# Score matmuls of a dilated attention layer: the low parts of the keys in 128-row tiles padded with zero rows

## The chip, the core and the metric

The kernel is one program on one core of a Trainium2 chip. The metric is the device time of one execution in microseconds (us); each number below is either such a time or was read from one execution that the hardware profiler recorded. Engine names: PE is the tensor engine (PEld its weight loads), DVE the vector engine, ACT the scalar engine, POOL GpSimd, SP the queue that issues the DMAs.

## The reference, cut to what matters

A trunk of four layers on 256 tokens of width 1024. Layer i has a mixer (retention, dilated attention, gMLP, retention), a SwiGLU channel mixer and a gated embedding. Only layer 1, the dilated attention, is touched. It has 16 heads of width 64 and three groups of window and dilation; each group has queries, keys and values of its own.

```python
qkv = (h @ w_in).reshape(B, S, 3, 3, 16, 64)
for gi, (window, dil) in enumerate(((128, 1), (512, 4), (2048, 16))):
    logits = einsum('qhd,khd->hqk', q, k) * 64 ** -0.5 + bias   # masked outside the window
    e = exp(logits - max); o = e @ v / sum(e); lse = max + log(sum(e))
w = softmax(lse over the three groups)
o = sum(w * o over the three groups);  return o @ w_out
```

The three groups together are one softmax over the logits of all three groups, and the kernel computes it so.

## The kernel before, in words

**Split operands.** Every float32 operand of a product is split into a high part (rounded by ACT to the format that PE multiplies in one pass, fp32r) and a low part (the rest, by DVE). A product is then three matmuls, high x high, high x low and low x high (`mm3`, L203 to L205). The weights stream in as chunks in a fixed order: SP loads them into `raw` (L146), ACT writes `wh` (L173), DVE writes `wl` (L174). The order of instructions on each engine is the order of the program text; which chunks are split where is set by a table of small numbers (`P`), and up to eight chunks are held split.

**The attention layer.** The loop runs over eight pairs of heads. For pair i PE does four chunks of the value projection (`token_major`, 12 matmuls of 384 columns for each chunk), and for each of the three groups a projection of queries and keys (`project`, 48 matmuls of 256 columns). Between these stand the steps of the pair before: `scores` of its even head after the third value chunk, `scores` of its odd head after the fourth, then, each after one of the three projections, the transposes of the probabilities (`turn_p`, L624) and the products with the values (`values`, L636 to L646). After the loop the last pair gets the same steps between the rows of the output projection.

**One call of `scores`.** There are 16 calls, one for each head. A call makes 12 matmuls in 6 couples: three of 256 columns (the later 128 queries against all keys, one for each group) and three of 128 columns (the earlier 128 queries). A couple adds into the same accumulator:

- L585 uses 128 rows. The stationary operand is `both[hh]`, in which the head's 64 rows hold the high part of the query and the other 64 rows hold its low part; the moving operand is `high[hh]`, which holds the high part of the key twice. One matmul gives high x high and low x high.
- L586 uses 64 rows, the head's own: the high part of the query against the low part of the key.

```python
both, high, low = p["qk"][g]
pe.matmul(dst, lhsT=both[hh][:, q], rhs=high[hh][:, k], start=True, stop=False)
pe.matmul(dst, lhsT=both[hh][part, q], rhs=low[part, k], start=False, stop=True)
```

`low` is one tile for each group, in which both heads of a pair have 64 rows each; DVE writes it in `project` (L677). DVE then adds the bias and finds the extreme of each row in three steps (L595, L598, L600), ACT takes the exponentials (L605, L607), DVE normalises (L613 to L616), PE transposes.

**Bias.** `load_bias` (L576) loads [128, 3, 256] for one head at the end of the loop body, two heads a pair, into a tag `bias` with two buffers. The tile `emb` ([128, 2, 1024]) lives through all layers: it holds the embedding of a layer from `Emb.unit` (written by ACT in the mixer, L381) to the evacuation of the gate (read by DVE, L1021). During the loop over the pairs it is not in use.

Of the kernel before, what the change touches and what calls it, by code (L numbers as in the profile page):

```python
# [9 lines left out]
F32 = mybir.dt.float32  # L10
F32R = mybir.dt.float32r
# [12 lines left out]
LEAD = 6  # L24
RAWS = 4
BIG = 1.0e30
# how many chunks of the weights are split at the named places, and (mt, ft) before how many of the last rows
# of a branch its first half of the tokens is transposed
P = dict(
    mt=1, mr0=0, mr1=1, mr2=0, mr3=2, mr4=0, mr5=1, m1=0, m2=1, m3=0, m4=0, m5=1, ft=2, fr0=1, fr1=1, fr2=0,  # L30
    fr3=1, fr4=0, fr5=1, f1=0, f2=1, f3=0, f4=0, f5=1, gq0=1, gq1=1, gq2=2, g1=2, g2=1, g3=0, g4=0, g5=0,
# [1 line left out]
)  # L33


# ---- the weights in the order in which they are used, a chunk per entry:
# (name, index, first row block, row blocks, columns); a chunk lies as [128 rows][row block][column]
def _cols(name, j, c0, n, nk, blocks=8):
    return [(name, j, k, nk, ((c0, n),)) for k in range(0, blocks, nk)]

# [67 lines left out]
def trunk(ctx: ExitStack, tc: tile.TileContext, x, p_t, norm_g, gcols, wts, rel_bias, gm_ln, gm_ws, gm_bs,  # L108
          c_ident, c_flip, c_rope, c_decay, c_onehot, c_mask, c_tril, out):
    nc = tc.nc  # L110
    act, dve, pe, dma = nc.scalar, nc.vector, nc.tensor, nc.sync
# [10 lines left out]
    def ps_tile(tag="ps"):  # L122
        return (psum if tag == "ps" else accp).tile([128, 512], F32, tag=tag, name=tag)

# [1 line left out]
    chunks, groups = [], []  # L126
    for l in range(DEPTH):
        off = 0
# [69 lines left out]
        def release(self):  # L198
            released.add(self.c)

# [1 line left out]
    def mm3(ps, lh, ll, rh, rl, start, stop):  # L202
        pe.matmul(ps, lhsT=lh, rhs=rh, start=start, stop=False)  # L203
        pe.matmul(ps, lhsT=lh, rhs=rl, start=False, stop=False)  # L204
        pe.matmul(ps, lhsT=ll, rhs=rh, start=False, stop=stop)  # L205

# [1 line left out]
    ident = const.tile([128, 128], F32, name="ident")  # L208
    ones = const.tile([128, 1], F32, name="ones")
    eps = const.tile([128, 1], F32, name="eps")  # L210
# [4 lines left out]
    emb = const.tile([128, 2, D], F32, name="emb")  # L215
# [28 lines left out]
    def cut(i, n=512):  # L244
        return slice(i * n, (i + 1) * n)

# [1 line left out]
    def turn(src, dst_hi, dst_lo, k0, tt, gain=None, tag="ps", wide=False):  # L248
        if gain is None:
            ps = ps_tile(tag)  # L250
# [46 lines left out]
            pe.matmul(ps[:, tok(tt)], lhsT=ones.to_broadcast([128, 128]), rhs=r[2][tt], start=True, stop=True)  # L297
        act.activation(out=r_b[:, 0, :], in_=ps[:, 0:256], func=AF.Copy)

# [1 line left out]
    def feature_major(name):  # L301
        ps = ps_tile()
        for b in range(2):
# [10 lines left out]
            mm3(ps, a_hi[:, kk, tok(tt)], a_lo[:, kk, tok(tt)], w.hi[:, k, :], w.lo[:, k, :], kk == 0, kk == 7)  # L314

    def token_whole(ps, ws, tt, then=None):
        """all chunks of a product, the parts of the activations that come last used last."""
        nk = 8 // len(ws)
        for kk in range(8):
            a, w, k = a_hi[:, kk, tok(tt)], ws[kk // nk], kk % nk  # L320
            pe.matmul(ps, lhsT=a, rhs=w.hi[:, k, :], start=kk == 0, stop=False)  # L321
            pe.matmul(ps, lhsT=a, rhs=w.lo[:, k, :], start=False, stop=False)  # L322
        for kk in range(8):
            w, k = ws[kk // nk], kk % nk
            pe.matmul(ps, lhsT=a_lo[:, kk, tok(tt)], rhs=w.hi[:, k, :], start=False, stop=kk == 7)  # L325
            if k == nk - 1:
                w.release()
                if then is not None:
                    then()
# [31 lines left out]
    def new_acc():  # L361
        return [[ps_tile("acc") for _ in range(2)] for _ in range(2)]

# [1 line left out]
    def split_p(t):  # L365
        act.activation(out=p_hi, in_=t, func=AF.Copy)
        dve.tensor_tensor(out=p_lo, in0=t, in1=p_hi.bitcast(F32), op=ALU.subtract)
# [16 lines left out]
                for w in self.w:  # L384
                    w.release()

# [1 line left out]
    def post_norm(tt, acc, gain, r):  # L388
        s = [sm(), sm()]
        for half in range(2):  # L390
# [12 lines left out]
            dve.tensor_tensor(out=h[:, tt, cut(half)], in0=h[:, tt, cut(half)], in1=t, op=ALU.add)  # L403

    def close_branch(late, acc, gain, r, l, n):
        """late: the row chunks whose second half of the tokens is still to come."""
        new = [None, None]
        act.preload_act_table(AF.Sqrt)
        K = "m" if n == 2 else "f"
        st["rate"] = 1  # L410
        post_norm(0, acc, gain, r)
        for i, (w, z, k) in enumerate(late):
            if i == len(late) - P[K + "t"]:
                turn_h(0, l, n)
            row(w, z, k, acc, False, i == len(late) - 1, (1,))
            w.release()
            pump(P[K + "r%d" % i])
        if P[K + "t"] == 0:
            turn_h(0, l, n)
        post_norm(1, acc, gain, r)  # L420
        pump(P[K + "1"])
        st["rate"] = P[K + "2"]

        def between():
            turn_h(1, l, n, True)
            pump(P[K + "3"])
            rms_of_h((0, 1), new)
            act.preload_act_table(AF.Silu if n == 2 else AF.Sigmoid)
            pump(P[K + "4"])
            st["rate"] = P[K + "5"]  # L430

        return new, between

# [1 line left out]
    def open_mixer(l, env, t):  # L435
        st["rate"] = P["rate"]
        dma.dma_start(out=t, in_=p_t[l].rearrange("(k p) t -> p k t", p=128))
# [128 lines left out]
    def attention(l, r, between, env):  # L566
        mp = env["pool"]
        name, wout = "attn_w_in", "attn_w_out"
        zf = mp.tile([128, 8, 256], F32, name="zf")
        flip = mp.tile([128, 128], F32, name="flip")  # L570
        dma.dma_start(out=flip, in_=c_flip)

        def load_bias(hd):
            t = mp.tile([128, 3, 256], F32, tag="bias", name="bias", bufs=2)
            v = vec[0, hd, :]
            dma.dma_start(out=t, in_=bass.AP(tensor=v.tensor, offset=v.offset, ap=[[1, 128], [16 * 384, 3], [1, 256]]))  # L576
            return t

        def scores(p, hh, tag="acc"):
            part = slice(64 * hh, 64 * hh + 64)  # L580
            s1, s2, s3 = ps_tile(tag), ps_tile(tag), ps_tile(tag)

            def logits(dst, g, q, k):
                both, high, low = p["qk"][g]
                pe.matmul(dst, lhsT=both[hh][:, q], rhs=high[hh][:, k], start=True, stop=False)  # L585
                pe.matmul(dst, lhsT=both[hh][part, q], rhs=low[part, k], start=False, stop=True)  # L586

            for g in range(3):
                logits((s1[:, 0:256], s1[:, 256:512], s2[:, 0:256])[g], g, tok(1), slice(0, 256))
            for g in range(3):  # L590
                logits(s3[:, cut(g, 128)], g, tok(0), tok(0))
            pr = mp.tile([128, 3, 384], F32, tag="pr", name="pr", bufs=2)
            bias = p["bias"][hh]
            m = [sm(), sm(), sm()]
            dve.tensor_tensor_reduce(out=pr[:, 0:2, 128:384], in0=s1.rearrange("p (g k) -> p g k", g=2),  # L595
                                     in1=bias[:, 0:2, :], scale=1.0, scalar=3.0e38, op0=ALU.add, op1=ALU.min,
                                     accum_out=m[0])
            dve.tensor_tensor_reduce(out=pr[:, 2, 128:384], in0=s2[:, 0:256], in1=bias[:, 2, :], scale=1.0,  # L598
                                     scalar=m[0], op0=ALU.add, op1=ALU.min, accum_out=m[1])
            dve.tensor_tensor_reduce(out=pr[:, :, 0:128], in0=s3[:, 0:384].rearrange("p (g k) -> p g k", g=3),  # L600
                                     in1=bias[:, :, 128:256], scale=1.0, scalar=3.0e38, op0=ALU.add, op1=ALU.min,
                                     accum_out=m[2])
            pump(P[("s%d" if p["p"] else "i%d") % hh] if p["p"] < 7 else 0)
            den = sm(2)
            act.activation(out=pr[:, :, 128:384], in_=pr[:, :, 128:384], func=AF.Exp, scale=-1.0, bias=m[1],  # L605
                           accum_out=den[:, 1:2])
            act.activation(out=pr[:, :, 0:128], in_=pr[:, :, 0:128], func=AF.Exp, scale=-1.0, bias=m[2],  # L607
                           accum_out=den[:, 0:1])
            return pr, den
# [42 lines left out]
        def project(p, g):  # L652
            ps = feature_major(name)
            if p["p"] == 0 and g == 0:
                spread(r)
            qk = mp.tile([128, 512], F32, tag="qk", name="qk")
            q = qk[:, 0:256].rearrange("p (a b) -> p a b", a=2)
# [3 lines left out]
                                     in0=ps[:, 0, :].rearrange("p (a b) -> p a b", a=2), scalar=-0.125,  # L661
                                     in1=r_b[:, 0, :].rearrange("p (a b) -> p a b", a=2), op0=ALU.mult, op1=ALU.mult)
            dve.tensor_tensor(out=qk[:, 256:512], in0=ps[:, 1, :], in1=r_b[:, 0, :], op=ALU.mult)
            both = [mp.tile([128, 256], F32R, tag=f"both{g}{hh}", name="both") for hh in range(2)]
            high = [mp.tile([128, 256], F32R, tag=f"high{g}{hh}", name="high") for hh in range(2)]
            low = mp.tile([128, 256], F32R, tag=f"low{g}", name="low")
            parts = (slice(0, 64), slice(64, 128))
            for hh in range(2):
                own, other = parts[hh], parts[1 - hh]
                act.activation(out=both[hh][own, :], in_=qk[own, 0:256], func=AF.Copy)  # L670
                act.activation(out=high[hh][own, :], in_=qk[own, 256:512], func=AF.Copy)
            for hh in range(2):
                own, other = parts[hh], parts[1 - hh]
                act.activation(out=high[hh][other, :], in_=qk[own, 256:512], func=AF.Copy)
                dve.tensor_tensor(out=both[hh][other, :], in0=qk[own, 0:256], in1=both[hh][own, :].bitcast(F32),
                                  op=ALU.subtract)
                dve.tensor_tensor(out=low[own, :], in0=qk[own, 256:512], in1=high[hh][own, :].bitcast(F32),  # L677
                                  op=ALU.subtract)
            p["qk"].append((both, high, low))

# [1 line left out]
        for i in range(8):  # L682
# [14 lines left out]
            p = {"p": i, "v": v, "qk": []}  # L697
# [198 lines left out]

        return compute

# [1 line left out]
    def ffn(l, r, between, env):  # L900
        fp = env["pool"]
        name, wout = "ffn_w_in", "ffn_w_out"
# [199 lines left out]
            r, between = embed_gate(l, r, between)  # L1102


# [1 line left out]
def _consts():  # L1106
    f = np.float32
    inv = (f(10000.0) ** (-np.arange(0, 256, 2, dtype=f) / f(256))).astype(f)
# [64 lines left out]
```

## Time and profile before

| what | us |
|---|---|
| median of three runs | 1769.78 (1768.28 to 1772.07) |
| span of the profiled execution, first to last instruction | 1768.2 |
| PE busy in it | 1759.0 (99%) |
| PEld busy | 1607.0 (91%) |
| DVE busy | 1141.7 (65%) |
| ACT busy | 985.1 (56%) |

The profiled execution's own time is its span, 1768.2 us, which lies 1.6 us under the median of the runs. Busy time of PE counts modelled ends of pipelined matmuls, which overlap, so a share of 99% says that PE hardly ever waits and not that each matmul goes as fast as it could. The distance from one matmul's start to the next one's, the pitch, tells more. PEclk in a view by stretches is the clock that was granted to the tensor engine, as a share of full speed (1.00 is 2.4 GHz, 0.50 is 1.2 GHz).

### The profile page before, as it was taken

The numbers are of one execution on the slowest core, as the hardware profiler recorded it, in microseconds if no ns is written. First come the engines' busy times: TensorE is split into PE (matmuls) and PEld (weight loads), VectorE is DVE, ScalarE is ACT, GpSimd is POOL, SyncE is SP. The second block draws the span as 40 slices with busy tenths as digits, with TensorE's granted clock in tenths as the row PEclk, the third lists the DMA queues.
The fourth block names the chain that finished last, engine by engine and source line by source line (L and its number), as shares of the span: only waits on it lengthen the run. The fifth ranks groups of instructions, "written<-read, shape, count | busy, mean of one in ns | idle before, by whom it ended". The sixth has DMA issues, their size and how long they took to land.

```text
span 1768.2 us, 27679 instructions
## 1 busy us (share of the span) xinstructions
PE 1759.0 (99%) x11411; PEld 1607.0 (91%) x11411; DVE 1141.7 (65%) x1670; ACT 985.1 (56%) x1515; POOL 0.2 (0%) x4
## 2 busy tenths in 40 slices
PE   9999999999999999999999999999999999999999
PEld 7888898999999999899999888899999888899998
DVE  7666665558777777775556775665557756675546
ACT  5645754348665656574445754654457555664435
POOL 0000000000000000000000000000000000000000
PEclk9999999999999999999999999999999999999999
DMA  7554564544545445356554654455545455455550
GB/s 288 210 190 155 180 218 166 206 162 169 173 148 138 144 149 162 92 192 212 182 188 167 224 195 184 167 205 200 183 164 182 175 186 183 174 203 192 179 202 24
DMA packets 53598, 314.32 MB, mean 178 GB/s; under 512 B 5632, under 2 KB 13616, under 8 KB 19168
## 3 DMA queue, kind: packets, MB, share of 16 engines
q1 hardware_dynamic: 53472, 312.56, 51.6%
q8 instruction: 89, 1.46, 0.3%
q14 instruction: 37, 0.30, 0.1%
HBM read 311.41 MB, written 1.12 MB: 177 GB/s over the span
## 4 chain that ended last, share of the span: by engine, by line
PE 96%; ACT 1%; DVE 1%; DMA 1%; issue 1%; SPq 0%; ACTq 0%; DVEq 0%
PE ps L203 21%; PE ps L204 20%; PE ps L205 20%; PE acc L203 8%; PE acc L205 8%; PE acc L204 8%; PE acc L586 1%; PE acc L585 1%; PE acc L261 1%; PE acc L624 1%; PE ps L252 1%; DMA raw<-in_w_dram 1%; PE acc L325 1%; PE acc L322 1%; PE acc L321 1%; ACT wh L173 1%
## 5 line engine op out<-in xcount | busy, mean ns | idle before, releaser
L174 DVE TENSOR_TENSOR wl<-raw,wh 128x1024 fp32r<-128x1024 f32 (+1 forms) x567 | 661.8, 1205 | 192.3 <-ACT wh L173 191.0
L173 ACT ACTIVATE wh<-raw 128x1024 fp32r<-128x1024 f32 (+1 forms) x567 | 565.3, 1040 | 178.1 <-PE ps L204 112.4
L203 PE MATMUL ps<-a_hi,wh 128*128 128x256 f32 x1792 | 514.2, 287 | 0.0
L204 PE MATMUL ps<-a_lo,wh 128*128 128x256 f32 x1792 | 510.9, 285 | 0.0
L205 PE MATMUL ps<-a_hi,wl 128*128 128x256 f32 x1792 | 510.8, 285 | 0.0
L203 PEld LDWEIGHTS ps<-a_hi,wh 128*128 128x128 f32 x1792 | 347.5, 194 | 2.6 <-issue 0.6
L204 PEld LDWEIGHTS ps<-a_lo,wh 128*128 128x128 f32 x1792 | 347.7, 194 | 1.4
L205 PEld LDWEIGHTS ps<-a_hi,wl 128*128 128x128 f32 x1792 | 347.3, 194 | 0.0
L203 PE MATMUL ps<-wh,a_hi 128*128 128x512 f32 (+2 forms) x776 | 268.6, 346 | 0.9 <-ACT wh L162 0.9
L204 PE MATMUL ps<-wl,a_hi 128*128 128x512 f32 (+2 forms) x776 | 266.7, 344 | 0.3 <-DVE wl L163 0.2
L205 PE MATMUL ps<-wh,a_lo 128*128 128x512 f32 (+2 forms) x776 | 266.6, 344 | 0.0
L203 PEld LDWEIGHTS ps<-wh,a_hi 128*128 128x128 f32 x776 | 147.5, 190 | 16.5 <-ACT wh L162 1.4
L204 PEld LDWEIGHTS ps<-wl,a_hi 128*128 128x128 f32 x776 | 147.7, 190 | 15.0 <-DVE wl L163 0.5
L205 PEld LDWEIGHTS ps<-wh,a_lo 128*128 128x128 f32 x776 | 147.8, 190 | 14.7
L203 PE MATMUL acc<-wh,hh 128*128 128x512 f32 x288 | 112.8, 392 | 0.0
L204 PE MATMUL acc<-wl,hh 128*128 128x512 f32 x288 | 112.4, 390 | 0.0
L205 PE MATMUL acc<-wh,hl 128*128 128x512 f32 x288 | 112.3, 390 | 0.0
L910 DVE TENSOR_TENSOR hid<-ps,gr 128x512 f32<-128x512 f32 x36 | 24.9, 691 | 99.6 <-PE ps L205 99.6
L913 ACT ACTIVATE hh<-hid 128x512 fp32r<-128x512 f32 x36 | 22.8, 632 | 101.7 <-DVE hid L910 101.7
L263 ACT ACTIVATE a_hi<-acc,gc 128x128 fp32r<-128x128 f32 x192 | 52.3, 382 | 39.8 <-PE acc L261 39.8
L205 PEld LDWEIGHTS acc<-wh,hl 128*128 128x128 f32 x288 | 54.1, 188 | 11.5
L203 PEld LDWEIGHTS acc<-wh,hh 128*128 128x128 f32 x288 | 54.2, 188 | 10.3
(205 smaller groups left out, 2203.4 us busy)
## 6 DMA issues: line engine op xcount, KB each, us to landing
raw<-in_w_dram SPq DMA_DIRECT2D x266, 1024.0 KB, 4.9
raw<-in_w_dram SPq DMA_DIRECT2D x16, 768.0 KB, 4.3
bias<-vec SPq DMA_DIRECT2D x16, 384.0 KB, 8.1
gain<-in_norm_g_dram SPq DMA_DIRECT2D x8, 512.0 KB, 6.7
ln<-in_gm_ln_dram SPq DMA_DIRECT2D x2, 1024.0 KB, 6.9
raw<-in_w_dram SPq DMA_DIRECT2D x3, 512.0 KB, 8.1
dec<-in_c_decay_dram SPq DMA_DIRECT2D x4, 384.0 KB, 5.6
h<-in_x_dram SPq DMA_DIRECT2D x4, 256.0 KB, 5.5
```

Source lines behind the costliest of these rows:

```text
L173: act.activation(out=hi[:, 0:n], in_=raw, func=AF.Copy)
L174: dve.tensor_tensor(out=lo[:, 0:n], in0=raw, in1=hi[:, 0:n].bitcast(F32), op=ALU.subtract)
L203: pe.matmul(ps, lhsT=lh, rhs=rh, start=start, stop=False)
L204: pe.matmul(ps, lhsT=lh, rhs=rl, start=False, stop=False)
L205: pe.matmul(ps, lhsT=ll, rhs=rh, start=False, stop=stop)
L252: pe.transpose(ps[:, cut(i, 128)], src[:, cut(i, 128)], ident)
L261: pe.transpose(ps[:, cut(i, 128)], src[:, cut(i, 128)], ident)
L263: act.activation(out=dst_hi[:, k0 + i, tok(tt)], in_=ps[:, cut(i, 128)], func=AF.Copy, scale=gain(k0 + i))
L321: pe.matmul(ps, lhsT=a, rhs=w.hi[:, k, :], start=kk == 0, stop=False)
L322: pe.matmul(ps, lhsT=a, rhs=w.lo[:, k, :], start=False, stop=False)
L910: dve.tensor_tensor(out=hd, in0=up, in1=gr, op=ALU.mult)
L913: act.activation(out=hh, in_=hd, func=AF.Copy)
```

## The change

`low` becomes `lows`: for each group and each head of a pair a tile of 128 rows, allocated once before the loop. The 64 rows that do not belong to the head are set to zero once, by six DVE memsets of 64 x 256 at the start of the layer. The second matmul of a couple then takes all 128 rows of `both[hh]`; the query's low part meets zeros. `project` writes the head's own 64 rows as before. The bias of an odd head is loaded into a part of `emb` that is not in use during the loop, and the tag `bias` has one buffer.

```diff
+        lows = [[mp.tile([128, 256], F32R, name=f"low{g}{hh}") for hh in range(2)] for g in range(3)]
+        for pair in lows:
+            for hh in range(2):
+                dve.memset(pair[hh][64 - 64 * hh:128 - 64 * hh, :].bitcast(F32), 0.0)
+
         def load_bias(hd):
-            t = mp.tile([128, 3, 256], F32, tag="bias", name="bias", bufs=2)
+            if hd % 2:
+                t = emb[:, 1, 0:768].rearrange("p (g k) -> p g k", g=3)
+            else:
+                t = mp.tile([128, 3, 256], F32, tag="bias", name="bias")
...
         def scores(p, hh, tag="acc"):
-            part = slice(64 * hh, 64 * hh + 64)
...
-                pe.matmul(dst, lhsT=both[hh][part, q], rhs=low[part, k], start=False, stop=True)
+                pe.matmul(dst, lhsT=both[hh][:, q], rhs=low[hh][:, k], start=False, stop=True)
...
-            low = mp.tile([128, 256], F32R, tag=f"low{g}", name="low")
+            low = lows[g]
...
-                dve.tensor_tensor(out=low[own, :], in0=qk[own, 256:512], in1=high[hh][own, :].bitcast(F32),
+                dve.tensor_tensor(out=low[hh][own, :], in0=qk[own, 256:512], in1=high[hh][own, :].bitcast(F32),
                                   op=ALU.subtract)
```

The rest of the diff takes comment lines out.

## Rows read from the trace of the kernel before

**Rows 1.** The profile's page: busy time of each engine; the chain that ended last.

```profile
PE 1759.0 (99%) x11411; PEld 1607.0 (91%) x11411; DVE 1141.7 (65%) x1670; ACT 985.1 (56%) x1515; POOL 0.2 (0%) x4
...
PE 96%; ACT 1%; DVE 1%; DMA 1%; issue 1%; SPq 0%; ACTq 0%; DVEq 0%
```

**Rows 2.** Waits of PE, whole span: us in total, times, longest.

```profile
PE ps L1078 <- DVE warm L1073: 1.5, 1, 1.5
```

**Rows 3.** Timeline of PE, one call of `scores`: start us, us, instruction.

```profile
697.42 0.33 PE L205 MATMUL ps<-wh,a_lo 128*128 128x384 f32 x1
697.59 0.28 PE L585 MATMUL acc<-high,both 128*128 128x256 f32 x1
697.80 0.38 PE L586 MATMUL acc<-low,both 64*128 64x256 f32 x1
698.11 0.38 PE L585 MATMUL acc<-high,both 128*128 128x256 f32 x1
...
699.36 0.33 PE L585 MATMUL acc<-high,both 128*128 128x128 f32 x1
699.61 0.32 PE L586 MATMUL acc<-low,both 64*128 64x128 f32 x1
...
700.88 0.44 PE L203 MATMUL ps<-wh,a_hi 128*128 128x384 f32 x1
701.16 0.34 PE L204 MATMUL ps<-wl,a_hi 128*128 128x384 f32 x1
```

**Rows 4.** Timeline of PE, matmuls that follow others of their own form.

```profile
706.72 0.28 PE L205 MATMUL ps<-a_hi,wl 128*128 128x256 f32 x1
706.84 0.28 PE L203 MATMUL ps<-a_hi,wh 128*128 128x256 f32 x1
...
487.16 0.52 PE L642 MATMUL ps<-th,v 128*64 128x128 f32 x6
487.52 0.28 PE L645 MATMUL ps<-tl,v 128*64 128x256 f32 x1
...
488.22 1.14 PE L624 MATMUL acc<-flip,pr 128*128 128x128 f32 x9
489.12 0.36 PE L203 MATMUL ps<-a_hi,wh 128*128 128x256 f32 x1
```

**Rows 5.** By stretches, one period of the loop each: us, busy us (count) by engine, PEclk, DMA.

```profile
462.53:502.50 39.97, 39.97 (x266) 37.28 (x265) 31.73 (x60) 26.56 (x50) 0.00 (x0) 0.91 0.54 166
502.50:540.89 38.39, 38.39 (x265) 35.79 (x265) 28.47 (x57) 23.65 (x46) 0.00 (x0) 0.96 0.47 145
540.89:580.82 39.93, 39.93 (x266) 37.19 (x265) 28.56 (x57) 23.65 (x46) 0.00 (x0) 0.91 0.48 139
```

**Rows 6.** By stretches again: a short one and the rest of the span.

```profile
466.52:469.93 3.41, 3.41 (x12) 3.04 (x10) 3.41 (x4) 2.68 (x7) 0.00 (x0) 0.50 0.45 109
...
671.32:1766.99 1095.67, 1091.51 (x7102) 997.80 (x7101) 693.06 (x961) 595.02 (x879) 0.00 (x0) 1.00 0.51 177
```

**Rows 7.** Waits of DVE from 440 to 760 us: us in total, times, longest.

```profile
DVE qk L660 <- PE ps L205: 24.8, 7, 3.9
```

**Rows 8.** Timeline of DVE at the layer's start and in its first scored pair.

```profile
434.04 1.22 DVE L174 TENSOR_TENSOR wl<-raw,wh 128x1024 fp32r<-128x1024 f32 x1 [0.76 <-ACT wh L173]
435.18 2.15 DVE L266 SCALAR_TENSOR_TENSOR a_lo<-acc,gc,a_hi 128x128 fp32r<-128x128 f32 x8
...
472.95 0.56 DVE L600 CUSTOM_DVE_ANT_1 pr<-acc,bias 128x384 f32<-128x384 f32 x1 [0.75 <-PE acc L586]
...
475.17 0.47 DVE L616 TENSOR_SCALAR pr<-pr,sm 128x384 f32<-128x384 f32 x1
```

**Rows 9.** A single line: count, duration in ns (min/median/max), first and last start.

```profile
L1073 DVE MEMSET warm<- x1: 485/485/485, 1.0 to 1.0; 128x512 uint32 x1
```

**Rows 10.** Timeline of SP, and the page's DMA list: KB, us to landing.

```profile
487.90 0.96 SPq L576 DMA_DIRECT2D bias<-vec  x2
...
bias<-vec SPq DMA_DIRECT2D x16, 384.0 KB, 8.1
```

## The prediction, made before the changed kernel was run

> **What bounds the kernel now.** I read the page first. PE is busy for 99% of the span and makes 96% of the chain that ended last [rows 1]. The list of PE's waits comes second: its longest entry is 1.5 us, at the very start [rows 2], and none of its entries lies in the attention layer. So in that layer nothing that DVE, ACT or the DMAs do holds PE; only what PE itself spends on each matmul counts. Busy time can't show that, so the third view is PE's timeline, read by pitch, the distance from start to start.
>
> Where matmuls of one form follow each other, a pitch is 0.12 us for 256 columns (706.72 to 706.84) [rows 4] and 0.17 us for 384 columns (697.42 to 697.59) [rows 3]. Inside a call of `scores` the 128-row and 64-row matmuls alternate, and there the pitch is 0.31 us from a 64-row matmul of 256 columns to the 128-row one behind it (697.80 to 698.11), and 0.25 us from a 128-row one of 128 columns to the 64-row one behind it (699.36 to 699.61) [rows 3]. The matmul behind the call pays too: 0.28 us from 700.88 to 701.16 in place of 0.17 [rows 3]. Accumulating into the same place can't be the reason, since the 0.12 us matmuls do that as well; what differs is the number of rows, and time is lost in both directions, 0.19 us in the first. A call takes 3.29 us (697.59 to 700.88) [rows 3].
>
> The fourth view is the granted clock by stretches. In the loop over the pairs it falls to 0.50, which is 1.2 GHz, for stretches of 3.41 us, the first from 466.52, just behind the first call [rows 6]; behind the last of these stretches it is 1.00 to the end of the span [rows 6]. A period of the loop has a mean clock of 0.91 and 39.9 us with two such stretches, 0.96 and 38.4 us with one [rows 5]. This alternates over six periods, so there are 3 x 2 + 3 x 1 = 9 stretches, and the seventh period has none.
>
> **The change part by part.**
>
> *The 96 second matmuls of the 16 calls become 128-row.* Then nothing in a call alternates. The six 256-column matmuls should take the 0.12 us of rows 4. For six 128-column ones of this type with 128 stationary columns the trace has no price. The nearest rows are 0.06 us with 64 stationary columns (six from 487.16 to 487.52) and 0.10 us for nine transposes with 128 stationary columns in another type (488.22 to 489.12) [rows 4]; above it stands the 0.12 us of 256 columns. I take 0.10, since what may last longer than 128 columns of data is the load of 128 stationary columns, which only that row has. A call is then 6 x 0.12 + 6 x 0.10 = 1.32 us. Before, it was 3.29 + (0.28 - 0.17) = 3.40 us. That is 2.08 us a call and 33.3 us in 16 calls; with 0.06 it is 2.32 and 37.1 us, with 0.12 it is 1.96 and 31.4 us.
>
> The Trainium skill, page "TensorE: Matmul & The Clock Gate", section "LDWEIGHTS (loading the stationary operand)", has the load take a time that grows with stationary columns alone; an estimate by its formula for 128 of them is 107 ns. By it a call would be 1.36 us and the 16 calls 32.6 us shorter; by the row of 0.06 us the load would not show at all. No run here shows it for this type yet.
>
> *The clock.* The stretches at 0.50 begin behind calls, and PE waits for nothing there, so I put them down to the slow pitch of the calls: in 3.3 us PE streams what it otherwise streams in 1.3 us. A call of 1.3 us amid full-rate matmuls should not pull the clock down. One stretch costs 39.93 - 38.39 = 1.54 us [rows 5], call it 1.5; nine make 13.5 us. The bounds are nothing and all of it.
>
> *DVE loses its slack.* A period without a half-clock stretch is 38.39 - 1.5 = 36.9 us, and after the change 36.9 - 2 x 2.08 = 32.7 us. DVE is busy for 28.5 us of each [rows 5], so its share goes from 74% to 87%. It now waits 24.8 us in seven periods for the first projection [rows 7]; this goes. Late next are the transposes of the even head, which need L616. In the first period DVE is behind with weight splits: L616 ends at 475.64, of which 0.75 us were a wait for scores [rows 8], so 474.9 after the change. PE would be there at 462.53 + 1.32 + 12 x 0.17 + 1.32 + 48 x 0.12 = 473.0. Cost: 1.9 us, once. In the other six periods I see no such wait, since DVE is ahead when they begin; bounds 0 and 1 us each, 6 us in all, and I take 0. Queued behind L616 on DVE are two weight splits and then the projection's evacuation, which PE's next scores need only at the end of the period.
>
> *The six memsets.* DVE writes 64 x 256 six times at the layer's start, between the splits of the first weights and `a_lo`, which PE needs next (L266 at 435.18) [rows 8]. The one large memset in the trace is 128 x 512 in 0.485 us [rows 9]; with half the columns I take 0.24 each, 1.45 us, less the 0.76 us in which DVE is idle there [rows 8]: 0.7 us. Bounds: 0 (PE has other matmuls meanwhile) and 6 x 0.485 = 2.9 us.
>
> *The odd head's bias in `emb`; one buffer for the tag.* Nothing. There are two places before and after, each with the same last reader, so SP issues both loads where it does now. They land 8.1 us after issue, and a load issued at 487.90 [rows 10] is read in the period that begins at 502.50 [rows 5]: 14.6 us of cover. Without cover it would cost the missing part of 8.1 us a pair. The gate of layer 0 has read `emb` before the layer begins, and `Emb.unit` writes these columns again only after the last odd head's scores. The number and place of DVE's writes of `low` stay.
>
> **Sum.** 33.3 + 13.5 - 1.9 - 0.7 = 44.2 us. From the profiled execution's own 1768.2 us that is 1724.0; it lies 1.6 us under the median of the runs, 1769.8, so the forecast for a median is 1725.6 us, 2.5% less.
>
> **Rivals.**
>
> *B, the clock falls as before.* If the half-clock stretches have another cause than the calls, 13.5 us don't come, and DVE keeps more slack: 1769.8 - 33.3 + 0.7 = 1737.2 us. For it speaks that some calls have no stretch behind them. Against it: none occurs in the 1096 us behind the loop [rows 6].
> The Trainium skill, same page, section "HAM oscillation — how this bites in real kernels", ties the fall of the clock to gaps in which PE is idle while it waits. By that rule there is no fall to be cured here, as PE waits for nothing in the loop; the rows at 0.50 show falls without such a gap, which the rule doesn't cover. Its time would be that of B.
>
> *C, DVE sets the pace of the loop.* DVE's 28.5 busy us and its short waits for ACT in each period may not fit in 32.7 us. One us a period and the dear ends of the memsets and of the 128-column matmuls give 31.4 + 13.5 - 1.9 - 6 - 2.9 = 34.1, so 1735.7 us. For it: a share of 87% with fixed order. Against it: DVE's longest waits are for PE [rows 7] and shrink by themselves.
>
> *D, the alternation of rows isn't what costs.* If the pitch of 0.31 us belongs to this couple of operands, the call stays at 3.3 us and the memsets cost at most 2.9: 1770 to 1773 us, no change that can be told. Against it: the 0.28 us of the innocent matmul behind the call [rows 3].
>
> *E, slower: the odd bias comes late.* If sharing `emb` held the loads of L576 on SP's queue, all weight loads behind them would be held too, and the odd head's L595 would wait. To eat 44.2 us, each of 8 loads must come 5.5 us after PE needs it, 14.6 - 8.1 + 5.5 = 12 us later than now; at 14 us later the time would be 1725.6 + 8 x 7.5 = 1786 us. For it: the buffer is one that other steps use. Against it: none of these runs in the loop.
>
> **Chances.** The forecast 0.70, B 0.13, C 0.08, D 0.05, E 0.04. Differences under 0.2% (3.5 us) can't be told from no change here. The first three are faster: 0.91; D is the same: 0.05; E is slower: 0.04. The forecast's own range is 1719 (0.06 us pitch, no DVE wait: 37.1 + 13.5) to 1731. To hold 8 in 10 it must reach to B and C, so 1717 to 1740 us.
>
> **What the profile after would show.** Pitches of 0.12 and about 0.10 us within a call; a call of 1.3 us; the matmul behind it at 0.17 us; a clock of 1.00 in every period; periods of about 32.7 us; one wait of PE for L616 in the first pair; DVE at 87% in the loop. I would be wrong if 128-row couples still took 0.31 us each, if 0.50 stretches stayed, if PE waited for DVE in each pair, or if L595 waited for a DMA.

## The result and the profile after

The changed kernel takes 1727.33 us (median of four runs, 1726.85 to 1727.5) against 1769.03 us for the kernel before in the runs beside it. The ratio is 0.9765 with a 95% interval of 0.9751 to 0.9779: 2.35% faster. The forecast was 1725.6 us, the range 1717 to 1740 us. The profiled execution's span went from 1768.2 to 1725.6 us, 42.6 us, where the sum had 44.2.

The page of the kernel after, busy time and the chain that ended last, which answer to [rows 1]:

```profile
PE 1714.1 (99%) x11411; PEld 1582.4 (92%) x11411; DVE 1140.8 (66%) x1676; ACT 982.8 (57%) x1515; POOL 0.2 (0%) x4
...
PE 97%; ACT 1%; DVE 1%; issue 0%; DMA 0%; ACTq 0%; SPq 0%
```

PE executes as many matmuls as before (11411), but is busy for 45 us less; the work of DVE and ACT is the same within 2.3 us, six instructions of DVE (the memsets) included. The lines of the couple are now L595 and L596, ten further down than L585 and L586.

One call of `scores` on PE's timeline, which answers to [rows 3]:

```profile
497.25 0.28 PE L595 MATMUL acc<-high,both 128*128 128x256 f32 x1
497.37 0.28 PE L596 MATMUL acc<-low,both 128*128 128x256 f32 x1
497.48 0.28 PE L595 MATMUL acc<-high,both 128*128 128x256 f32 x1
...
497.96 0.22 PE L595 MATMUL acc<-high,both 128*128 128x128 f32 x1
498.01 0.28 PE L596 MATMUL acc<-low,both 128*128 128x128 f32 x1
498.13 0.27 PE L595 MATMUL acc<-high,both 128*128 128x128 f32 x1
498.24 0.27 PE L596 MATMUL acc<-low,both 128*128 128x128 f32 x1
...
498.57 0.39 PE L203 MATMUL ps<-wh,a_hi 128*128 128x384 f32 x1
498.80 0.34 PE L204 MATMUL ps<-wl,a_hi 128*128 128x384 f32 x1
```

The pitch of 256 columns is 0.12 us (497.25 to 497.37), the pitch of 128 columns 0.11 us (498.13 to 498.24), and the call takes 1.32 us (497.25 to 498.57), as forecast. That the two agree to the hundredth is in part luck: 0.11 us was forecast as 0.10, and the first matmul of 128 columns has a pitch of only 0.05 us (497.96 to 498.01). The matmul behind the call has 0.23 us, not the 0.17 that the forecast expected.

The weight loads (PEld) show what changed between the matmuls. First three loads of a call of the kernel before [rows 3], then three of the kernel after:

```profile
697.42 0.19 PEld L585 LDWEIGHTS acc<-high,both 128*128 128x128 f32 x1
697.80 0.18 PEld L586 LDWEIGHTS acc<-low,both 64*128 64x128 f32 x1 [0.19 <-issue]
698.11 0.19 PEld L585 LDWEIGHTS acc<-high,both 128*128 128x128 f32 x1
...
497.08 0.19 PEld L595 LDWEIGHTS acc<-high,both 128*128 128x128 f32 x1
497.25 0.19 PEld L596 LDWEIGHTS acc<-low,both 128*128 128x128 f32 x1
497.37 0.19 PEld L595 LDWEIGHTS acc<-high,both 128*128 128x128 f32 x1
```

In the kernel before, the load for a matmul with another number of rows starts together with its own matmul (697.80, 698.11) and not during the one ahead. In the kernel after it starts 0.12 us earlier, together with the matmul ahead (the load at 497.25 belongs to the matmul at 497.37).

The loop by stretches, one period each from one even head's scores to the next, which answers to [rows 5] (us; busy us of PE, PEld, DVE, ACT, POOL with counts; clock; DMA share and GB/s):

```profile
462.87:497.25 34.38, 33.12 (x266) 32.95 (x265) 31.03 (x60) 25.93 (x50) 0.00 (x0) 1.00 0.61 192
497.25:530.19 32.94, 32.94 (x266) 32.94 (x265) 28.55 (x57) 23.72 (x47) 0.00 (x0) 1.00 0.56 169
530.19:563.13 32.94, 32.94 (x266) 32.94 (x265) 28.20 (x57) 23.33 (x46) 0.00 (x0) 1.00 0.58 168
```

The clock is 1.00 in every period, a period is 32.94 us from the second on where it was 38.4 to 40.0, and DVE is busy for 86 to 87% of it. Only the first period has idle time of PE, 34.38 - 33.12 = 1.26 us. The waits of PE over the whole span (us in total, times, longest) name it in their third row, and answer to [rows 2]:

```profile
PE acc L261 <- DMA h<-in_x_dram: 2.0, 2, 1.7
PE ps L1088 <- DVE warm L1083: 1.5, 1, 1.5
PE acc L634 <- issue: 1.3, 1, 1.3
PE acc L261 <- DVE h L403: 1.1, 2, 0.7
...
PE acc L203 <- ACT a_hi L734: 0.2, 1, 0.2
```

The longest wait lies at the span's start and was 1.0 us before; when the layer begins both kernels are level again (the L261 transposes ahead of it start at 425.32 us before and at 425.30 after). L634 are the first transposes. The view puts this wait down to "issue"; DVE's timeline of the kernel after shows what stands in front of them:

```profile
466.44 3.49 DVE L174 TENSOR_TENSOR wl<-raw,wh 128x1024 fp32r<-128x1024 f32 x3
469.85 1.13 DVE L699 SCALAR_TENSOR_TENSOR v<-ps,sm,v 128x384 fp32r<-128x384 f32 x2
470.90 0.68 DVE L605 CUSTOM_DVE_ANT_0 pr<-acc,emb 128x512 f32<-128x512 f32 x1
...
474.35 0.47 DVE L626 TENSOR_SCALAR pr<-pr,sm 128x384 f32<-128x384 f32 x1
```

The last step of the normalisation (L626, before L616) ends at 474.82 and the transposes begin at 474.92. DVE doesn't wait between 461.30 and there; three weight splits, the odd head's scores and a fourth split (472.62, 0.95 us) stand in its queue ahead of the normalisation.

### The profile page after: what moved, and what is told of

Its sections match the earlier page's. It is cut to its first block, busy times and chain, and to the rows that moved or that the text cites. A ratio compares the mean times of both kernels' runs of the same rounds, so it can differ in the third digit from the quotient of the medians.

```text
span 1725.6 us, 27686 instructions
## 1 busy us (share of the span) xinstructions
PE 1714.1 (99%) x11411; PEld 1582.4 (92%) x11411; DVE 1140.8 (66%) x1676; ACT 982.8 (57%) x1515; POOL 0.2 (0%) x4
## 4 chain that ended last, share of the span: by engine, by line
PE 97%; ACT 1%; DVE 1%; issue 0%; DMA 0%; ACTq 0%; SPq 0%
PE ps L203 21%; PE ps L204 21%; PE ps L205 21%; PE acc L203 8%; PE acc L205 8%; PE acc L204 8%; PE acc L261 1%; PE ps L252 1%; PE acc L634 1%; PE acc L325 1%; PE acc L322 1%; PE acc L321 1%; PE acc L596 1%; PE ps L321 1%; PE ps L325 1%; PE acc L595 1%
## 5 line engine op out<-in xcount | busy, mean ns | idle before, releaser
L203 PEld LDWEIGHTS ps<-a_hi,wh 128*128 128x128 f32 x1792 | 343.4, 192 | 2.0 <-issue 0.6
L204 PEld LDWEIGHTS ps<-a_lo,wh 128*128 128x128 f32 x1792 | 343.5, 192 | 1.3
L205 PEld LDWEIGHTS ps<-a_hi,wl 128*128 128x128 f32 x1792 | 343.4, 192 | 0.0
```

## The experiments

**Theory.** Each change of the number of rows between neighbouring matmuls costs PE time; a call that is slow for this reason pulls the granted clock down behind it. **Rivals.** A 64-row matmul is slow by itself; the bias or the tiles carry part of the gain; the clock falls for a reason of its own, or because rows change. Every kernel below is the changed one with an edit, computes the same result and was timed against the kernel before.

**The rows alone undone.**

```diff
-                pe.matmul(dst, lhsT=both[hh][:, q], rhs=low[hh][:, k], start=False, stop=True)
+                part = slice(64 * hh, 64 * hh + 64)
+                pe.matmul(dst, lhsT=both[hh][part, q], rhs=low[hh][part, k], start=False, stop=True)
```

> The changed kernel with only the rows undone: the second matmul of each couple again takes the head's own 64 rows, everything else (padded tiles, memsets, bias of odd heads in emb) stays. Theory (the alternation of 128 and 64 rows is what costs, and the slow calls bring the half clock): the whole gain goes, 1769 us within 2, calls of 3.3 us, about nine stretches at clock 0.50. Rival (the bias or the tiles carry part of the gain): clearly under 1766 us.

Measured: 1770.14 us, ratio 1.0009 (0.9996 to 1.0021), so no difference from the kernel before. By stretches:

```profile
462.41:502.33 39.92, 39.92 (x266) 37.34 (x265) 31.74 (x60) 26.54 (x50) 0.00 (x0) 0.91 0.54 166
502.33:542.25 39.92, 39.92 (x265) 37.16 (x265) 28.56 (x57) 23.65 (x46) 0.00 (x0) 0.91 0.45 139
```

Nine stretches at 0.50 came back, two in each of these periods. The whole gain is in the rows of L596. The six memsets, the tiles and the bias in `emb` together cost nothing that can be told here.

**64 rows, but grouped.** In each call the six 128-row matmuls come first and the six 64-row ones behind them; `dsts`, `qs` and `ks` list the same accumulators, queries and keys as before.

```diff
...
-            for g in range(3):
-                logits((s1[:, 0:256], s1[:, 256:512], s2[:, 0:256])[g], g, tok(1), slice(0, 256))
-            for g in range(3):
-                logits(s3[:, cut(g, 128)], g, tok(0), tok(0))
+            part = slice(64 * hh, 64 * hh + 64)
...
+            for i in range(6):
+                both, high, low = p["qk"][i % 3]
+                pe.matmul(dsts[i], lhsT=both[hh][:, qs[i]], rhs=high[hh][:, ks[i]], start=i in (0, 2, 3), stop=False)
+            for i in range(6):
+                both, high, low = p["qk"][i % 3]
+                pe.matmul(dsts[i], lhsT=both[hh][part, qs[i]], rhs=low[hh][part, ks[i]], start=False, stop=i in (1, 2, 5))
```

> The changed kernel with 64-row second matmuls again, but in each call the six 128-row matmuls come first and the six 64-row ones after them: one change of rows into the group and one out of it in place of twelve. Theory (each change of rows costs 0.15 to 0.19 us): a call of about 1.33 + 0.35 = 1.7 us, 5 to 6 us in all, 1732 to 1734 us, clock 1.00 throughout. Rival (a 64-row matmul is itself slow, 0.25 to 0.31 us): a call of about 2.3 to 2.4 us, 16 us or more in all, 1743 us or more, with some stretches at 0.50.

Measured: 1730.61 us, ratio 0.9793 (0.9779 to 0.9808), clock 1.00. One call on PE's timeline, and its weight loads:

```profile
496.85 0.80 PE L598 MATMUL acc<-high,both 128*128 128x256 f32 x6
497.57 0.91 PE L601 MATMUL acc<-low,both 64*128 64x256 f32 x6
498.41 0.44 PE L203 MATMUL ps<-wh,a_hi 128*128 128x384 f32 x1
498.69 0.34 PE L204 MATMUL ps<-wl,a_hi 128*128 128x384 f32 x1
...
496.68 0.83 PEld L598 LDWEIGHTS acc<-high,both 128*128 128x128 f32 x6
497.57 0.77 PEld L601 LDWEIGHTS acc<-low,both 64*128 64x128 f32 x6
498.41 0.19 PEld L203 LDWEIGHTS ps<-wh,a_hi 128*128 128x128 f32 x1
```

A call takes 1.56 us (496.85 to 498.41), only 0.24 us more than with padded rows, though half of its matmuls have 64 rows. So a 64-row matmul is not slow by itself. Two changes of rows, in and out, cost 0.24 us; in the kernel before twelve cost 3.29 - 1.32 = 1.97 us, 0.16 each on average. The cost isn't the same for each: 0.31 - 0.12 = 0.19 us where the matmuls have 256 columns and 0.25 - 0.11 = 0.14 us where they have 128 [rows 3]. The loads agree: the two at the changes (497.57 and 498.41) start together with their own matmuls, the others ahead of theirs. The sign and the mechanism of the theory hold, its size for this case (0.35 us a call) was too high. The rival with 1743 us or more falls. The Trainium skill has a rule for this: "TensorEngine Tiling (Array Packing)", section "Key Properties", says that changing the tiling mode drains the tensor engine, while changing the tile alone does not. The trace agrees, with 0.12 us for a change here and 0.14 to 0.19 us in the kernel before.

**64 rows for odd heads only.**

```diff
+                part = slice(64, 128) if hh else slice(0, 128)
+                pe.matmul(dst, lhsT=both[hh][part, q], rhs=low[hh][part, k], start=False, stop=True)
```

> The changed kernel with 64-row second matmuls in the calls of odd heads alone (8 of 16). Theory: 8 x 2.0 = 16 us for the pitch, plus the half-clock stretches that 8 slow calls bring; before, two slow calls in a period brought one or two stretches, so 3 to 8 stretches of 1.5 us: 1748 to 1755 us, each stretch behind an odd call. Rival (the clock falls for another cause than the slow calls): stretches also behind even calls, or none, 1743 us.

Measured: 1747.39 us, ratio 0.989 (0.9873 to 0.9906), just below the forecast's lower end, with three stretches. The odd call of the first pair lasts from 466.51 to 469.81; by stretches:

```profile
463.01:466.51 3.50, 3.50 (x26) 3.50 (x25) 3.35 (x7) 2.48 (x4) 0.00 (x0) 1.00 0.67 188
466.51:470.43 3.92, 3.92 (x18) 2.66 (x18) 3.92 (x6) 3.92 (x8) 0.00 (x0) 1.00 0.64 209
470.43:473.84 3.41, 3.41 (x19) 3.41 (x18) 3.23 (x11) 1.41 (x4) 0.00 (x0) 0.50 1.02 396
```

The first row holds the even call with padded rows, at full clock; the second the odd one; the third is the half clock, 0.6 us behind its end. The other two stretches, at 542.11 and 647.92, also begin within 1 us after an odd call, and none follows an even one; five of the eight odd calls have no stretch behind them. The span is 1744.8 us: 19.2 more than with all rows padded, of which 8 x 2.0 = 16.0 are pitch and 3 x 1.5 = 4.5 clock, less the 1.3 us wait of the first period, which isn't there.

**Half the columns.** Each couple of 128 columns becomes two couples of 64 columns, all with 128 rows.

```diff
             for g in range(3):
-                logits(s3[:, cut(g, 128)], g, tok(0), tok(0))
+                for c in range(2):
+                    logits(s3[:, 128 * g + 64 * c:128 * g + 64 * c + 64], g, tok(0), slice(64 * c, 64 * c + 64))
```

> The changed kernel with each couple of 128 columns made as two couples of 64 columns, 12 matmuls in place of 6 in each call, the same arithmetic. Theory (a matmul of 128 columns at 0.11 us waits for the load of its 128 stationary columns, so half the columns take the same time): 6 x 0.11 = 0.66 us a call more, 10.6 us in all, 1738 us. Rival (its time goes with the columns): about 0.05 us each, under 1 us in all, 1727 to 1729 us.

Measured: 1735.41 us, ratio 0.9818 (0.9804 to 0.9833). On PE's timeline:

```profile
497.89 0.28 PE L596 MATMUL acc<-low,both 128*128 128x64 f32 x1
498.00 0.28 PE L595 MATMUL acc<-high,both 128*128 128x64 f32 x1
498.11 0.28 PE L596 MATMUL acc<-low,both 128*128 128x64 f32 x1
```

A matmul of 64 columns has the pitch of one of 128, 0.11 us. A call grew by 0.64 us (1.96 after 1.32), as the theory had it; the span grew by 7.9 us instead of 10.2, in part because the wait of the first period is gone. So what a 128-column matmul of this kind waits for is not its columns. This agrees with the formula of the Trainium skill, page "TensorE: Matmul & The Clock Gate", section "LDWEIGHTS (loading the stationary operand)", by which the load of 128 stationary columns takes 107 ns as an estimate. It agrees with the pitch alone: each load is recorded with 0.19 us, and two loads overlap. The row of 0.06 us [rows 4] had 64 stationary columns.

**A slow call without any change of rows.** Quarters instead of halves: 24 matmuls of 32 columns, all of 128 rows.

```diff
             for g in range(3):
-                logits(s3[:, cut(g, 128)], g, tok(0), tok(0))
+                for c in range(4):
+                    logits(s3[:, 128 * g + 32 * c:128 * g + 32 * c + 32], g, tok(0), slice(32 * c, 32 * c + 32))
```

> The changed kernel with each couple of 128 columns made as four couples of 32 columns: 24 matmuls in place of 6 in each call, all of 128 rows, the same arithmetic. At the 0.11 us that the halves showed, a call is 0.7 + 24 x 0.11 = 3.4 us, as long as a call of the kernel before, and it streams the same columns, but no row count changes in it. Theory (the clock falls because PE streams little during a slow call): 6 to 10 stretches at 0.50 come back, and the time is 1727 + 16 x 2.0 + 9 to 14 = 1768 to 1773 us. Rival (the change of rows itself pulls the clock down): clock 1.00, 1757 to 1760 us.

Measured: 1768.45 us, ratio 0.9992 (0.9977 to 1.0006), eight stretches in the loop. The odd call of the first pair lasts from 468.16 to 471.47. Three of the 32-column matmuls of another call, and the stretches:

```profile
503.72 0.26 PE L595 MATMUL acc<-high,both 128*128 128x32 f32 x1
503.83 0.26 PE L596 MATMUL acc<-low,both 128*128 128x32 f32 x1
503.95 0.26 PE L595 MATMUL acc<-high,both 128*128 128x32 f32 x1
...
461.00:472.40 11.40, 11.40 (x91) 11.40 (x90) 10.67 (x19) 8.11 (x13) 0.00 (x0) 1.00 0.65 237
472.40:475.81 3.41, 3.41 (x19) 3.41 (x18) 3.38 (x9) 2.36 (x5) 0.00 (x0) 0.50 0.66 267
475.81:501.09 25.28, 25.28 (x207) 25.28 (x207) 19.18 (x37) 17.53 (x34) 0.00 (x0) 1.00 0.48 136
```

This kernel is as slow as the one before although no row count changes in its calls: a call is 3.31 us again, and the half clock is back. PE and PEld are marked busy for the whole of every stretch. So the clock falls with calls in which PE takes 3.3 us to stream what it otherwise streams in 1.3 us, whatever makes them slow. The rival by which the change of rows pulls the clock itself falls.

**The small losses.** First the memsets on the idle GpSimd (`nc.gpsimd.memset` for `dve.memset`).

> The changed kernel with the six memsets on GpSimd in place of DVE. Theory (the memsets delay a_lo on DVE and PE waits 0.3 us for it): the eight L325 matmuls at the layer's start take 1.39 us as before in place of 1.73, the span is 0.3 us shorter. Rival (the 0.3 us has another cause): 1.7 us again.

The eight L325 matmuls took 1.39 us again (437.08 to 438.46), against 1.73 in the changed kernel; the span of this single run is 1725.1 us against 1725.6. The kernel after had this on DVE's timeline, which answers to [rows 8]:

```profile
433.36 2.08 DVE L578 MEMSET low<- 64x256 f32 x6
435.37 1.15 DVE L174 TENSOR_TENSOR wl<-raw,wh 128x1024 fp32r<-128x1024 f32 x1
436.44 2.14 DVE L266 SCALAR_TENSOR_TENSOR a_lo<-acc,gc,a_hi 128x128 fp32r<-128x128 f32 x8
```

`a_lo` comes 1.26 us later than before, and 0.34 us of this reach PE. Then the same with fewer splits in front of the first transposes, beside the unaltered changed kernel on the same chip.

```diff
-    rate=1, s0=2, s1=1, i0=2, i1=1, ar0=0, ar1=0, ar2=1, a0=0, a1=1,
+    rate=1, s0=2, s1=1, i0=0, i1=1, ar0=0, ar1=0, ar2=1, a0=0, a1=1,
```

> The changed kernel with the memsets on GpSimd and with i0 = 0 in the table P: no weight split is put behind the first even head's scores on DVE, which then reaches L616 of that head earlier. Theory (DVE is late by its weight splits in the first pair): the 1.3 us wait of PE ahead of the first transposes goes, later splits catch up, and the time is 1.5 us under the changed kernel, 0.1%. Rival (the splits that were left out are missed later): the wait moves to a weight, no gain or a loss.

> The changed kernel unaltered, on the same chip as the others: 1727 us within 2; it is what the kernel with the memsets on GpSimd and i0 = 0 is compared with.

1728.07 us with the edit and 1727.81 without, ratios 0.9759 (0.9745 to 0.9774) and 0.9759 (0.9744 to 0.9773): no gain. PE's wait ahead of the transposes was 1.5 us. DVE's timeline of the edited kernel shows the miss:

```profile
467.59 1.22 DVE L174 TENSOR_TENSOR wl<-raw,wh 128x1024 fp32r<-128x1024 f32 x1 [2.17 <-ACT wh L173]
```

The split that the value chunk asks for has its `wh` made behind ACT's exponentials now, and DVE stands 2.17 us for it. The theory that fewer splits alone would do it was wrong. The last try left one split there and took out the one ahead of the normalisation (`i0=1, i1=0`).

> The changed kernel with the memsets on GpSimd and with i0 = 1, i1 = 0 in the table P: one weight split fewer behind the first even head's scores, whose wh is made before ACT's exponentials, and none ahead of that head's normalisation. Theory (DVE reaches L616 of the first pair one split, 0.95 us, earlier): the wait of PE ahead of the first transposes falls from 1.3 to about 0.4 us, and the span to 1724.3 us or less; the median stays within the uncertainty, 1726 to 1728 us. Rival (again only the order changes and the split is missed elsewhere): 1.3 us or more of wait.

1727.47 us, ratio 0.977 (0.9756 to 0.9783). The waits of PE over the span:

```profile
PE acc L634 <- DVE pr L626: 0.5, 1, 0.5
...
PE acc L634 <- PE ps L205: 0.4, 1, 0.4
```

The first wait fell from 1.3 to 0.5 us, about as expected, but a second one of 0.4 us came at the odd head's transposes, and the span is 1726.1 us, not the 1724.3 or less that was expected. No version was found that beats the changed kernel by more than can be told.

## Why the prediction was right

*What costs* was read rightly, with one weak step. That couples of different row counts cost PE time between its instructions is shown by the rows alone undone (all of the gain lost) and by the grouped kernel (two changes instead of twelve, 0.24 us instead of 1.97). The weight loads show what is lost: at a change the load doesn't run during the matmul ahead. The argument against rival D, that the matmul behind the call paid too [rows 3], was half wrong: with no change of rows that matmul still has 0.23 us, so only 0.05 of its 0.28 us belonged to the change of rows. What stands against D is the kernel with the rows alone undone.

*Calls.* The step "3.29 + (0.28 - 0.17) = 3.40 us" is the term that was mis-sized: it should have left 0.23 for the matmul behind. Measured, a call and this matmul went from 3.57 to 1.55 us, 2.02 us, 32.3 us in 16 calls in place of 33.3 (for an odd call, 3.30 + 0.22 against 1.33 + 0.17 us, it is the same). Of the three prices for a 128-column matmul (0.06, 0.10, 0.12) the lowest was wrong; the measured 0.11 us lies between the chosen one and the highest, and the reason given, the load of 128 stationary columns, fits the halves.

*Clock.* All nine stretches are gone. Six periods took 235.1 us before and would have taken six times 32.94 + 2 x 2.02 = 36.98 us at full clock, so the stretches cost 13.2 us in place of 13.5. That calls of 3.3 us cause them is shown by the quarters, without a change of rows. So rival B falls. The rule of the Trainium skill that was cited with it (page "TensorE: Matmul & The Clock Gate", section "HAM oscillation — how this bites in real kernels"), which ties the fall of the clock to gaps in which PE is idle, doesn't cover this kernel: the clock fell while PE was marked busy throughout (with modelled ends), and no longer fell when the calls were faster. Two readings of the forecast need a correction. Six of the nine stretches begin behind a call; the other three (510.89, 589.40 and 667.91) begin within the last 0.6 us of an odd call. And the 1096 us of [rows 6] begin at 671.32, inside the loop, and hold four calls of 3.3 us, so a slow call doesn't always bring a stretch. What decides it stays open.

*DVE's slack.* Forecast 1.9 us once in the first period, measured 1.3 us at that place and nothing in the next ones. DVE was done at 474.82 (forecast 474.9); PE was there at 474.92 - 1.26 = 473.66 and not at 473.0, which makes the wait shorter. There was no other wait in the loop, so rival C didn't come, though DVE's share is the 87% that was forecast.

*Memsets.* Forecast 0.7 us, measured 0.34 us, shown by moving them. They last 2.08 us where 1.45 was forecast, but PE has other matmuls for most of the delay.

*What was not in the sum* is the last pair behind the loop. Its first call took 1.86 us in place of 1.33, the twelve matmuls behind it 3.16 us where the same twelve behind the second call took 2.79, and the last transposes 1.16 us in place of 0.90: 1.2 us. On the list of PE's waits 0.2 us of this are put down to `a_hi` (L734, ACT). The timelines show what else ends just before PE goes on: the first call's third couple starts at 691.95, behind DVE's read of an accumulator for `zf` (L660, to 691.90); the third matmul behind that call at 693.98, behind DVE's `a_lo` (L735, to 693.92); the seventh of the nine last transposes at 707.80, behind L660 again, which ends at 707.74 like ACT's evacuation of the embedding (L381). So PE now comes there sooner than DVE and ACT; that these releases are the cause is argued from the times, and no run tests it. The sum is then 32.3 + 13.2 - 1.3 - 0.3 - 1.2 = 42.7 us against 42.6 in the span. Against the forecast's 44.2 us, two gains came out 1.0 and 0.3 us smaller and a loss of 1.2 us was not foreseen, while 0.6 and 0.4 us of the forecast losses didn't come: that the total is off by only 1.6 us is in part luck.

*Bias in `emb`.* Nothing, as forecast, and rival E fell: the loads into `emb` landed 8.1 to 10.6 us after issue (median 9.0), and no instruction on the list of DVE's waits in the layer waited for a DMA.

## What to carry to other kernels

On a tensor engine that is busy all the time, read pitches, not busy time: matmuls that alternate between row counts lost 0.14 to 0.19 us at each change here, where the next weights were not loaded during the matmul ahead, and padding with zero rows, or grouping by row count, got nearly all of it back. Price a saving of pitch together with the clock, since a stage that streams slowly, as the calls of 3.3 us did, can pay again in the stage behind it. When one stage gets faster, look up what the next engine has queued in its first and last round, for the steady rounds in between may hide what those don't.

## What was not expected of the hardware

A call without any change of rows, with PE marked busy throughout, brought the 1.2 GHz stretches back as soon as it was slowed to 3.31 us by matmuls of 32 columns; calls of 1.32, 1.56 and 1.96 us had none. A matmul of 32, 64 or 128 columns with 128 stationary columns had the same pitch of 0.11 us, so the small ones gave nothing for their size.
